# SSD value products in four groups of 32 queries, NSA compression with operands swapped, HGRN steps spread wider

## The chip, the core and the metric

One core of a Trainium2 chip runs the whole program in one launch. The measure is the device time of that launch in microseconds; lower is better. The engines that matter here are TensorE (PE, matrix products; its weight loads have a row PEld of their own), VectorE (DVE), ScalarE (ACT) and the queue on SyncE (SP) that issues the loads.

## What is computed

A first block of two layers (a feed-forward net, a mixer, a second feed-forward net; the mixer is an SSD scan in layer 0 and a pooling mixer in layer 1) is followed by a second block of two layers, in which an HGRN2 recurrence and a native sparse attention (NSA) share the projections of one input. There are 256 tokens (and 256 context tokens in the first block) of width 1024, all in float32. The change touches three places:

```python
# SSD, per chunk of 128, direction and group of 8 heads:
cb = jnp.einsum('bclgn,bcsgn->bclsg', Cc, Bc)
y_diag = jnp.einsum('bclsg,bclsge,bcsgep->bclgep', cb, Lmat, xdt)

# HGRN2, per chunk: decayed scores of queries and keys, then values
attn = jnp.einsum('bhtk,bhsk,bhtsk->bhts', q_, k_, jnp.exp(diff))
o_intra = jnp.einsum('bhts,bhsv->bhtv', attn, v_)

# NSA compression: 15 blocks of 32 tokens, step 16, for each of 2 groups
idx = jnp.arange(n_cmp)[:, None] * CMP_STRIDE + jnp.arange(CMP_BLOCK)[None, :]
blocks = kv[:, idx] + pos_emb[None, None, :, None, :]
flat = blocks.transpose(0, 1, 3, 2, 4).reshape(B, n_cmp, G, CMP_BLOCK * D)
return jax.nn.silu(flat @ w1 + b1) @ w2
```

## The kernel before

**Dense products.** Nearly all of PE's time goes into projections whose weights are streamed from memory once. A load on SP's queue brings raw float32 weights (`wraw`); `prepare` splits them into a rounded high part on ACT (`whi`, L68) and the rest on DVE (`wlo`, L69); PE then makes each product in three passes (`mm3`, L299 to L301; `tm_chunk`, L1173 to L1175). A feature-major projection tile (`fm_tile`, tile `pfm`) is 24 matmuls of 256 columns; its result leaves the PSUM bank by a DVE multiply with the norm factor.

**Order.** The program is written in generators that are interleaved, and a tile scheduler adds the waits; each engine works its own list in that order. `bank` hands out PSUM banks from three tags: five "mm", two "co", one "st".

**SSD core (`core`, one generator for each of 4 groups of 8 heads).** For two halves i of the queries and two directions `d_` the decay matrix `M[i, d_]` (128 keys x 8 heads x 128 queries) is loaded from memory, turned into exponents on ACT (Relu, L666) or DVE, exponentiated (L700) and multiplied by the scores (`cbm`). There are four M buffers in all, so the next group's load waits for the last reader of a buffer. The last reader is `py` (L725): for each head and direction one matmul with the 128x128 piece of M as weights and 64 columns of `xd` moving. Then `yt` takes the sum on DVE (L727), is transposed (`pgy`), gated, and its squares are summed for a norm: `stacc`, `stsq` on ACT and DVE, then `st` on PE (L340). The generators of the groups run beside the projections of the next ones (`px`, `pz`, `pB`, `pC`).

**HGRN2 (`hgrn(half)`, 4 heads each).** Nine terms `(128, 0, 16, 8, 4, 2, 1, 64, 32)` are worked in a pipeline of three steps: `prepare` (DVE makes `z` from the cumulated decays, ACT exponentiates it, DVE multiplies queries and keys in, L1277 to L1287), `score` (PE makes `ps` from z; L1296 for the far term, L1308 for the near terms in four tiles of 32, L1331 for 64 and 32) and `values` (PE, `po`). Near scores are collected in `near` by a multiply with a mask (L1314) and predicated copies (L1317), then spread into `at` (L1323) before the term 64 is scored. After the last term come a sum of squares on PE (`st`, L1365), Ln and exp on ACT, and `on` on DVE (L1367).

**NSA.** `project_nsa` makes `ck` and `cv` (256 tokens for each of 2 groups, with 32 position vectors behind them), then runs `project_more` (keys, values, gates and queries, tiles `kk`, `vv`, `png`, `nq`, with a rope after every second one) with a side chain: `compress("k")`, `compress("v")`, `compressed_out()`, one side step for every second main step (`between`). `compress` adds 32 matmuls in two groups of 16 into `pc`: the weight is `w1[:, j, :]` (128 columns), and 45 columns move (15 blocks of either group, and the position vectors). Each has a bias (`cb`, L1396) and a silu (`s1`, L1398). `compressed_out` makes the compressed keys (`pkc`, `kcmp`, their rope through `pkr`) and values (`vrep`, `pvc`, `vc`). The attention (`nsa`) starts with copies of `kcmp` into `kk` (L1512) and the first scores `psc` (L1532).

**The interleaving.** `run_with(main, side, per)` takes one step of the main generator (the last four query projections of HGRN, then `project_nsa`) and then `per` steps of the side generator (both HGRN halves) on the mean:

```python
run_with(chain(project_q(range(4, 8)), project_nsa()), chain(hgrn(0), hgrn(1)), 2.6)
```

Of the kernel before, what the change touches and what calls it, by code (L numbers as in the profile page):

```python
# [10 lines left out]
F32 = mybir.dt.float32  # L11
# [6 lines left out]
P = 128  # L18
T = 256
# [70 lines left out]
def build(ctx: ExitStack, tc, a, out):  # L90
# [22 lines left out]
    def nm(s):  # L113
        uid[0] += 1
        return f"{s}{uid[0]}"
# [284 lines left out]
    def run_with(main_steps, side_steps, per):  # L400

        due = 0.0
        for _ in main_steps:
            due += per
            while due >= 1.0:
                due -= 1.0
                next(side_steps, 0)
        for _ in side_steps:
            pass

    def ssd_phase(uh, ul, Rx, norm, tail):
        with tc.tile_pool(name="ssd", bufs=1) as sp:
# [234 lines left out]
            def core(g):  # L647
# [55 lines left out]
                for i in range(2):  # L703
                    po = []
                    for d_ in range(2):
                        po.append(bank("co", nm("pyo")))
                        TE.matmul(po[d_], CT[:, P * i:P * i + P], Hst[d_][i ^ d_], start=True, stop=True)
                    xd = [weighted(X[:, 2 + i, :], dt[:, 2 + i, hs[d_]]) for d_ in range(2)]
                    yield
                    yv = yt[:, i, :]  # L710
                    V.tensor_tensor(heads(yv), heads(po[0]), col64(ea[:, i, hs[0]]), op=OP.mult)
                    t = sp.tile([P, 512], F32, tag="xw", name=nm("yx"), bufs=4)
                    V.tensor_tensor(heads(t), heads(po[1]), col64(ea[:, i, hs[1]]), op=OP.mult)
                    V.tensor_add(yv, yv, t)
                    yield
                    for d_ in range(2):
                        V.tensor_tensor(M[i, d_], M[i, d_], cbm[d_][:, i:i + 1, :].to_broadcast([P, 8, P]), op=OP.mult)
                        yield
                    t = weighted(X[:, 2 + i, :], dsk[:, 8 * g:8 * g + 8])
                    V.tensor_add(yv, yv, t)  # L720
                    yield
                    py = bank("co", nm("py"))
                    for h in range(8):
                        for d_ in range(2):
                            TE.matmul(py[:, 64 * h:64 * h + 64], M[i, d_][:, h, :], xd[d_][:, 64 * h:64 * h + 64],  # L725
                                      start=d_ == 0, stop=d_ == 1)
                    V.tensor_add(yv, yv, py)  # L727
                    yield

# [448 lines left out]
    def fm_tile():  # L1178
        p = bank("mm", nm("pfm"))
        dense_tile(p[:, :T], W.next(), 0, KD, xh, xl, T)  # L1180
        return p[:, :T]
# [11 lines left out]
    def block2(l, norm, tail):  # L1193
        if True:
# [59 lines left out]
            def hgrn(half):  # L1254
# [34 lines left out]
                def score(m):  # L1289
                    c = terms[m]  # L1290
                    p = bank("mm", nm("ps"))
                    z = zs.get(m)
                    if c == P:
                        pv = p.rearrange("p (h t) -> p h t", t=P)
                        for h in range(4):
                            TE.matmul(pv[:, h], z[:, h, :P], z[:, h, P:], start=True, stop=True)  # L1296
                        sc["far"] = mx.tile([P, 4, P], F32, tag="h2", name=nm("far"), bufs=4)
                        S.activation(sc["far"], pv, AF.Copy)
                        return
                    if c < 32:  # L1300

                        for h in range(4):
                            for i in range(2):
                                for b in range(4):
                                    ts = slice(P * i + 32 * b, P * i + 32 * b + 32)
                                    lk, lq = ((z[:, h, ts], z[:, h, ts]) if c else
                                              (kT[:, h0 + h, ts], qT[:, h0 + h, ts]))
                                    TE.matmul(p[32 * b:32 * b + 32, 64 * h + 32 * i:64 * h + 32 * i + 32], lk, lq,  # L1308
                                              start=True, stop=True)
                        pv = p[:, :256].rearrange("p (n t) -> p n t", t=32)  # L1310
                        sh = [P, 8, 32]
                        if not c:
                            sc["near"] = mx.tile([P, 8, 32], F32, tag="near", name=nm("near"), bufs=2)
                            V.tensor_tensor(sc["near"], pv, own.unsqueeze(1).to_broadcast(sh), op=OP.mult)  # L1314
                        else:
                            n = PAIRS.index(c)
                            V.copy_predicated(sc["near"], pairs[:, n:n + 1, :].to_broadcast(sh), pv)  # L1317
                        return
                    if c == 64:

                        sc["at"] = mx.tile([P, 8, P], F32, tag="h2", name=nm("at"), bufs=4)
                        sh = [P, 8, 4, 32]
                        V.tensor_tensor(sc["at"].rearrange("p n (b t) -> p n b t", t=32),  # L1323
                                        sc["near"].unsqueeze(2).to_broadcast(sh),
                                        hmask.unsqueeze(1).unsqueeze(3).to_broadcast(sh), op=OP.mult)
                    n = P // (2 * c)
                    for h in range(4):
                        for i in range(2):
                            for e in range(n):
                                k0 = 2 * c * e  # L1330
                                TE.matmul(p[k0:k0 + c, c * (2 * h + i):c * (2 * h + i) + c],  # L1331
                                          z[:, h, P * i + k0:P * i + k0 + c], z[:, h, P * i + k0 + c:P * i + k0 + 2 * c],
                                          start=True, stop=True)
                    for e in range(n):
                        ks, qs = slice(2 * c * e, 2 * c * e + c), slice(2 * c * e + c, 2 * c * e + 2 * c)
                        S.activation(sc["at"][ks, :, qs], p[ks, :8 * c].rearrange("p (n t) -> p n t", t=c), AF.Copy)
# [44 lines left out]
            def compress(s):  # L1381

                x = nt["c" + s]
                w1 = None
                p = bank("mm", nm("pc1"))
                for e in range(2):
                    w1 = mx.tile([P, 16, P], F32, tag="kt", name=nm("w1"))
                    nc.sync.dma_start(w1, a["w1_" + s][l][:, 16 * e:16 * e + 16])
                    yield
                    for j in range(16):  # L1390

                        TE.matmul(p[:, :45], w1[:, j, :], bass.AP(tensor=x.tensor, offset=x.offset + 16 * e + j,
                                                                  ap=[x.ap[0], [T, 3], [16, 15]]),
                                  start=e == 0 and j == 0, stop=e == 1 and j == 15)
                b = mx.tile([P, 1], F32, tag="cb" + s, name=nm("cb"))
                V.tensor_add(b, p[:, 30:31], small["b1_" + s])  # L1396
                s1 = mx.tile([P, 30], F32, tag="s1" + s, name=nm("s1"), bufs=1)
                S.activation(s1, p[:, :30], AF.Silu, bias=b)  # L1398
                nt["s1" + s] = s1

            def compressed_out():

                reps = []
                for g in range(2):
                    r = mx.tile([P, 4, 32], F32, tag="vrep", name=nm("vrep"), bufs=2)
                    V.memset(r, 0.0)
                    V.tensor_copy(r[:, :, :15], nt["s1v"][:, 15 * g:15 * g + 15].unsqueeze(1).to_broadcast([P, 4, 15]))
                    reps.append(r)
# [27 lines left out]

            def project_nsa():
                for s in "kv":
                    t = mx.tile([P, 3, T], F32, name=nm("c" + s), tag="c" + s)
                    nt["c" + s] = t  # L1440
                    nc.sync.dma_start(t[:, 2, :32], a["pos_" + s][l])
                    V.memset(t[:, 2, 32:], 0.0)
                    for g in range(2):
                        V.tensor_mul(t[:, g], fm_tile(), R)
                        yield
                yield from between(project_more(), chain(compress("k"), compress("v"), compressed_out()), 2)

# [39 lines left out]
                S.activation(gates, p[:, :48], AF.Sigmoid)  # L1487
                nt["gates"] = gates

            run_with(chain(project_q(range(4, 8)), project_nsa()), chain(hgrn(0), hgrn(1)), 2.6)  # L1490


            gT = [(xh[:, :, T + 4:], xl[:, :, T + 4:]), (xh[:, :, :T], xl[:, :, :T])]
# [329 lines left out]
```

## Time and profile before

| what | us |
|---|---|
| median of 3 runs | 1966.04 |
| lowest and highest run | 1956.83, 1968.94 |
| profiled execution, its own time | 1965.64 |
| its span in the profile | 1963.9 |
| PE busy in it | 1914.9 |
| DVE busy | 1451.9 |
| ACT busy | 1042.0 |

The span is what the trace covers; its own time is 1.7 us longer. SSD's stretch lies at about 405 to 745 us of the span, the two HGRN/NSA stretches at about 1400 to 1500 (layer 0 of the second block) and 1718 to 1820 (layer 1). A float32 matmul shows as two records, so counts of records are twice the counts of matmuls. A record's own length covers its way through the array and overlaps its neighbours; what it costs PE is the distance from start to start. PEclk, the granted clock, is 1.00 at 2.4 GHz and 0.50 at 1.2 GHz.

### The profile page before, as it was taken

Reading aid. Unit: us, or ns where it says so; the run is one execution under the profiler, and the core shown is the slowest. Engines: PE = TensorE matmul, PEld = TensorE weight load, DVE = VectorE, ACT = ScalarE, POOL = GpSimd, SP = SyncE. Lnnn points to the kernel's source line nnn. Section 1 sums busy time; section 2 is a strip of 40 time slices with the busy share of each in tenths; the row PEclk is TensorE's granted clock in tenths of the full one; section 3 lists DMA queues with packets and bytes.
Section 4 is the critical chain, followed back from the end, with each engine's and each line's share of the span. In section 5 each row is a group of like instructions: output and inputs, shape, how many; then the busy total and the mean of one; then the engine's idle time right before and its main releaser. Section 6 shows DMA issues by size and latency. Waiting matters only on the chain.

```text
span 1963.9 us, 35899 instructions
## 1 busy us (share of the span) xinstructions
PE 1914.9 (98%) x14800; PEld 1744.2 (89%) x14800; DVE 1451.9 (74%) x2683; ACT 1042.0 (53%) x1629; POOL 0.2 (0%) x4
## 2 busy tenths in 40 slices
PE   8999999999999999999999999999999999989998
PEld 3888888897777799999999999999999998989987
DVE  5897788678887789865776587666776856586874
ACT  5332222366766666554555455557554756655573
POOL 0000000000000000000000000000000000000000
PEclk9999999999999999999999999999999999999999
DMA  7767788544323338645554545556434353525332
GB/s 314 260 240 285 274 310 320 186 141 132 88 71 143 107 129 324 245 161 204 178 188 163 203 148 175 171 195 192 152 125 168 108 169 133 194 70 197 133 108 87
DMA packets 81924, 353.03 MB, mean 180 GB/s; under 512 B 12416, under 2 KB 30912, under 8 KB 51040
## 3 DMA queue, kind: packets, MB, share of 16 engines
q1 hardware_dynamic: 81760, 350.73, 51.5%
q8 instruction: 116, 1.90, 0.4%
q14 instruction: 48, 0.39, 0.1%
HBM read 348.80 MB, written 1.12 MB: 178 GB/s over the span
## 4 chain that ended last, share of the span: by engine, by line
PE 89%; DVE 4%; ACT 4%; DMA 2%; issue 1%; SPq 0%; DVEq 0%; ACTq 0%
PE po L299 6%; PE po L301 6%; PE po L300 6%; PE pg L301 5%; PE pu L301 5%; PE pg L300 5%; PE pu L300 5%; PE pg L299 5%; PE pu L299 5%; PE pfm L299 3%; PE pfm L300 3%; PE pfm L301 3%; PE ptm L1173 2%; PE ptm L1174 2%; PE ptm L1175 2%; DMA M<-arow_d 2%
## 5 line engine op out<-in xcount | busy, mean ns | idle before, releaser
L68 ACT ACTIVATE whi<-wraw 128x1024 fp32r<-128x1024 f32 (+1 forms) x485 | 504.2, 1041 | 694.5 <-PE po L300 195.8
L69 DVE TENSOR_TENSOR wlo<-wraw,whi 128x1024 fp32r<-128x1024 f32 (+1 forms) x485 | 581.1, 1199 | 185.9 <-ACT whi L68 184.7
L301 PE MATMUL pg<-xh,wlo 128*128 128x258 f32 (+1 forms) x704 | 219.9, 312 | 0.1
L301 PE MATMUL pu<-xh,wlo 128*128 128x258 f32 (+1 forms) x704 | 219.9, 312 | 0.0
L300 PE MATMUL pg<-xl,whi 128*128 128x258 f32 (+1 forms) x704 | 219.0, 311 | 0.0
L299 PE MATMUL pg<-xh,whi 128*128 128x258 f32 (+1 forms) x704 | 218.5, 311 | 0.4 <-ACT xh L367 0.4
L300 PE MATMUL pu<-xl,whi 128*128 128x258 f32 (+1 forms) x704 | 218.7, 311 | 0.0
L300 PE MATMUL po<-hl,whi 128*128 128x256 f32 (+1 forms) x704 | 218.6, 311 | 0.0
L299 PE MATMUL po<-hh,whi 128*128 128x256 f32 (+1 forms) x704 | 218.6, 311 | 0.0
L301 PE MATMUL po<-hh,wlo 128*128 128x256 f32 (+1 forms) x704 | 218.6, 311 | 0.0
L299 PE MATMUL pu<-xh,whi 128*128 128x258 f32 (+1 forms) x704 | 218.2, 310 | 0.0
L234 DVE SCALAR_TENSOR_TENSOR adascr<-adaraw,csb 128x1024 f32<-128x1024 f32 x152 | 185.7, 1222 | 26.6 <-DMA adaraw<-in_ada 24.6
L299 PE MATMUL pfm<-xh,whi 128*128 128x256 f32 x640 | 189.3, 296 | 0.0
L300 PE MATMUL pfm<-xl,whi 128*128 128x256 f32 x640 | 184.6, 288 | 0.0
L301 PE MATMUL pfm<-xh,wlo 128*128 128x256 f32 x640 | 182.1, 285 | 0.0
L299 PEld LDWEIGHTS pg<-xh,whi 128*128 128x128 f32 x704 | 133.6, 190 | 8.6 <-ACT xh L367 0.6
L300 PEld LDWEIGHTS po<-hl,whi 128*128 128x128 f32 x704 | 133.8, 190 | 8.1
L301 PEld LDWEIGHTS po<-hh,wlo 128*128 128x128 f32 x704 | 133.8, 190 | 8.1
L299 PEld LDWEIGHTS po<-hh,whi 128*128 128x128 f32 x704 | 133.8, 190 | 8.1
L299 PEld LDWEIGHTS pu<-xh,whi 128*128 128x128 f32 x704 | 133.6, 190 | 7.8
L300 PEld LDWEIGHTS pg<-xl,whi 128*128 128x128 f32 x704 | 133.0, 189 | 7.9
L301 PEld LDWEIGHTS pg<-xh,wlo 128*128 128x128 f32 x704 | 132.9, 189 | 8.1 <-DVE wlo L69 0.3
(444 smaller groups left out, 4233.5 us busy)
## 6 DMA issues: line engine op xcount, KB each, us to landing
wraw<-in_ffn_gu SPq DMA_DIRECT2D x88, 1024.0 KB, 4.9
adaraw<-in_ada SPq DMA_DIRECT2D x64, 1024.0 KB, 6.5
wraw<-in_w SPq DMA_DIRECT2D x60, 1024.0 KB, 4.9
wraw<-in_ffn_d SPq DMA_DIRECT2D x24, 960.0 KB, 4.7
wraw<-in_ssd_wi SPq DMA_DIRECT2D x20, 1024.0 KB, 4.9
wraw<-in_w_out SPq DMA_DIRECT2D x16, 1024.0 KB, 5.1
wraw<-in_ffn_d SPq DMA_DIRECT2D x24, 448.0 KB, 3.2
adan<-in_ada_n SPq DMA_DIRECT2D x8, 1024.0 KB, 7.7
```

Source lines behind the costliest of these rows:

```text
L68: nc.scalar.activation(hi[:, :n], raw[:, o:o + n], AF.Copy)
L69: nc.vector.tensor_sub(lo[:, :n], raw[:, o:o + n], hi[:, :n].bitcast(F32))
L234: V.scalar_tensor_tensor(scr, t[:, h, :], 1.0, csb[s], op0=OP.mult, op1=OP.mult, accum_out=macc[l, s][:, n:n + 1])
L299: TE.matmul(o, wh, xh, start=start, stop=False)
L300: TE.matmul(o, wh, xl, start=False, stop=False)
L301: TE.matmul(o, wl, xh, start=False, stop=stop)
L1173: TE.matmul(o, h, wh[:, sl], start=k == 0, stop=False)
L1174: TE.matmul(o, h, wl[:, sl], start=False, stop=False)
L1175: TE.matmul(o, l, wh[:, sl], start=False, stop=k == KD - 1)
```

## The change

In SSD each of the 16 matmuls of `py` becomes four, with 32 query columns of M as weights each, which write 32 partitions of the result. In the compression the operands change places: 32 columns of x (step 16, both groups and the position columns) are the weights, `w1` (128 columns) moves, and four tokens j go into four groups of 32 partitions. The four partial sums are copied out by ACT (`part`), a yield follows, and one more matmul with the matrix `own` adds them in a new bank (`pc2`). For that the layout of `ck` and `cv` changes, and each projection tile leaves by two multiplies of 240 columns where one of 256 was. `near` has one buffer for two; `vrep` lies in another pool under the tag of `stsq`. `run_with` takes 1.9 side steps per main step for 2.6.

```diff
+                            for q in range(0, P, 32):
+                                TE.matmul(py[q:q + 32, 64 * h:64 * h + 64], M[i, d_][:, h, q:q + 32],
+                                          xd[d_][:, 64 * h:64 * h + 64], start=d_ == 0, stop=d_ == 1)
-                            TE.matmul(py[:, 64 * h:64 * h + 64], M[i, d_][:, h, :], xd[d_][:, 64 * h:64 * h + 64],
-                                      start=d_ == 0, stop=d_ == 1)
...
-                            sc["near"] = mx.tile([P, 8, 32], F32, tag="near", name=nm("near"), bufs=2)
+                            sc["near"] = mx.tile([P, 8, 32], F32, tag="near", name=nm("near"), bufs=1)
...
-                        TE.matmul(p[:, :45], w1[:, j, :], bass.AP(tensor=x.tensor, offset=x.offset + 16 * e + j,
-                                                                  ap=[x.ap[0], [T, 3], [16, 15]]),
-                                  start=e == 0 and j == 0, stop=e == 1 and j == 15)
+                        q = 32 * (j % 4)
+                        TE.matmul(p[q:q + 32, :P], bass.AP(tensor=x.tensor, offset=x.offset + 496 * e + j,
+                                                           ap=[x.ap[0], [16, 32]]),
+                                  w1[:, j, :], start=e == 0 and j < 4, stop=e == 1 and j > 11)
+                part = tmp.tile([P, P], F32, tag="t1k", name=nm("part"), bufs=2)
+                S.activation(part, p[:, :P], AF.Copy)
+                yield
+                p = bank("mm", nm("pc2"))
+                TE.matmul(p[:, :32], part, own, start=True, stop=True)
                 b = mx.tile([P, 1], F32, tag="cb" + s, name=nm("cb"))
-                V.tensor_add(b, p[:, 30:31], small["b1_" + s])
+                V.tensor_add(b, p[:, 15:16], small["b1_" + s])
...
-                    r = mx.tile([P, 4, 32], F32, tag="vrep", name=nm("vrep"), bufs=2)
+                    r = tmp.tile([P, 4, 32], F32, tag="stsq", name=nm("vrep"), bufs=2)
...
                     for g in range(2):
-                        V.tensor_mul(t[:, g], fm_tile(), R)
+                        p = fm_tile()
+                        for e in range(2):
+                            V.tensor_mul(t[:, e, 256 * g:256 * g + 240], p[:, 16 * e:16 * e + 240],
+                                         R[:, 16 * e:16 * e + 240])
...
-            run_with(chain(project_q(range(4, 8)), project_nsa()), chain(hgrn(0), hgrn(1)), 2.6)
+            run_with(chain(project_q(range(4, 8)), project_nsa()), chain(hgrn(0), hgrn(1)), 1.9)
```

How the lists of instructions move is shown at three places. The first is PE at the end of the first HGRN half of layer 0: `ps` are scores, `pfm` with its `whi` a projection tile, of which the first of its 24 rows stands here, `po` the values. Before:

```order
L1308 MATMUL ps1304_14446<-z21299_14367 32x32 x32
L1308 MATMUL ps1306_14485<-z21301_14407 32x32 x32
L299 MATMUL pfm1307_14519<-xh_93,whi356_14336 128x256
...
L1308 MATMUL ps1309_14557<-z21305_14480 32x32 x32
L299 MATMUL pfm1311_14594<-xh_93,whi357_14417 128x256
...
L1331 MATMUL ps1313_14630<-z21308_14551 64x64 x8
L1331 MATMUL ps1315_14642<-z21312_14624 32x32 x16
L299 MATMUL pfm1316_14661<-xh_93,whi358_14520 128x256
...
L1347 MATMUL po1286_14173<-at1314_14631,vt1272_13824 128x128 x4
```

And now:

```order
L1310 MATMUL ps1305_14864<-z21301_14785 32x32 x32
L299 MATMUL pfm1307_14901<-xh_93,whi357_14755 128x256
...
L1310 MATMUL ps1309_14937<-z21304_14858 32x32 x32
L299 MATMUL pfm1310_14971<-xh_93,whi358_14826 128x256
...
L1310 MATMUL ps1312_15010<-z21308_14932 32x32 x32
L299 MATMUL pfm1314_15045<-xh_93,whi359_14902 128x256
...
L1333 MATMUL ps1316_15081<-z21311_15004 64x64 x8
L299 MATMUL pfm1318_15093<-xh_93,whi360_14972 128x256
...
L1333 MATMUL ps1322_15134<-z21315_15075 32x32 x16
L299 MATMUL pfm1323_15153<-xh_93,whi361_15046 128x256
...
L1349 MATMUL po1286_14557<-at1317_15082,vt1272_14208 128x128 x4
```

Before, six projection tiles stand from the near scores of the first term (`ps1293`) to the values, and twice two scores follow each other directly; now each score has a tile behind it, and the values stand nine tiles after the far scores.

The second place is DVE just ahead of the attention of layer 0. `nq` and `z` are projections leaving their banks, `rsw` and `nq` the steps of a rope, `kcsw` and `kcmp` that of the compressed keys, `vcmp` the masked compressed values. Before:

```order
L69 TENSOR_TENSOR wlo377_15675<-wraw201_15426,whi377_15674 128x1024
L1502 TENSOR_TENSOR vcmp1395_15742<-vc1383_15592,b_head_mask_13393 128x512
L1475 TENSOR_TENSOR nq1365_15366<-pfm1388_15637,rstd_2_13492 128x256
L1424 TENSOR_TENSOR kcsw1390_15669<-pkr1389_15667,b_ropec_s_13381 32x30
L1425 TENSOR_TENSOR kcmp1382_15590<-kcmp1382_15590,b_ropec_c_13379 32x30
L69 TENSOR_TENSOR wlo378_15714<-wraw202_15525,whi378_15713 128x1024
L1189 TENSOR_TENSOR rsw1387_15631<-rsw1387_15631,b_rope_s_13377 32x512
L1190 TENSOR_TENSOR nq1365_15366<-nq1365_15366,b_rope_c_13375 32x512
L1426 TENSOR_TENSOR kcmp1382_15590<-kcmp1382_15590,kcsw1390_15669 32x30
L1475 TENSOR_TENSOR nq1365_15366<-pfm1391_15673,rstd_2_13492 128x256
L1191 TENSOR_TENSOR nq1365_15366<-nq1365_15366,rsw1387_15631 32x512
L1512 COPY kk1321_14716<-kcmp1382_15590 128x15 x2
```

And now:

```order
L1516 TENSOR_TENSOR vcmp1399_16138<-vc1392_16094,b_head_mask_13777 128x512
L1369 SCALAR_TENSOR_TENSOR on1280_14518<-po1332_15263,b_hnorm_13779,r1379_15997 128x512
L1433 TENSOR_TENSOR kcsw1396_16103<-pkr1395_16101,b_ropec_s_13765 32x30
L1434 TENSOR_TENSOR kcmp1391_16092<-kcmp1391_16092,b_ropec_c_13763 32x30
L1516 TENSOR_TENSOR vcmp1399_16138<-vc1392_16094,b_head_mask_13777 128x512
L1435 TENSOR_TENSOR kcmp1391_16092<-kcmp1391_16092,kcsw1396_16103 32x30
L69 TENSOR_TENSOR wlo379_16159<-wraw202_15797,whi379_16158 128x1024
L1191 TENSOR_TENSOR rsw1389_16084<-rsw1389_16084,b_rope_s_13761 32x512
L1192 TENSOR_TENSOR nq1348_15542<-nq1348_15542,b_rope_c_13759 32x512
L1642 TENSOR_TENSOR z1397_16107<-pfm1398_16108,rstd_2_13876 128x256
L1193 TENSOR_TENSOR nq1348_15542<-nq1348_15542,rsw1389_16084 32x512
L1526 COPY kk1313_15044<-kcmp1391_16092 128x15 x2
```

The copy into `kk` now stands behind the last `on` of HGRN, which was 34 rows ahead of it before, and behind a `z` that comes from the projection tile after `pkr`.

The third is PE at the same place, with `pkr` (the rope product of the compressed keys) and `psc` (the first scores of the attention); of each projection tile the first row stands here. Before:

```order
L1392 MATMUL pc11352_15236<-cv1310_14591,w11367_15413 128x45 x16
L299 MATMUL pfm1378_15520<-xh_93,whi371_15422 128x256
...
L299 MATMUL pfm1380_15558<-xh_93,whi372_15465 128x256
...
L1411 MATMUL pkc1381_15588<-s11351_15234,wc2_k1282_14137 128x30
L1418 MATMUL pvc1384_15593<-wc2_v1284_14141,vrep1376_15514 128x128
L1418 MATMUL pvc1385_15596<-wc2_v1284_14141,vrep1377_15517 128x128
L299 MATMUL pfm1386_15599<-xh_93,whi373_15521 128x256
...
L299 MATMUL pfm1388_15637<-xh_93,whi374_15559 128x256
...
L1422 MATMUL pkr1389_15667<-kcmp1382_15590,b_rot_13383 32x30
L299 MATMUL pfm1391_15673<-xh_93,whi375_15600 128x256
...
L299 MATMUL pfm1394_15712<-xh_93,whi376_15638 128x256
...
L1532 MATMUL psc1399_15751<-kk1321_14716,nq1365_15366 128x143
```

And now:

```order
L1402 MATMUL pc21382_16034<-own_13784,part1372_15916 128x32
L1367 MATMUL st1387_16047<-sq1378_15996,ones_91 128x512
L299 MATMUL pfm1388_16052<-xh_93,whi375_15931 128x256
...
L1420 MATMUL pkc1390_16090<-s11352_15577,wc2_k1282_14521 128x30
L1427 MATMUL pvc1393_16095<-wc2_v1284_14525,vrep1385_16040 128x128
L1427 MATMUL pvc1394_16098<-wc2_v1284_14525,vrep1386_16043 128x128
L1431 MATMUL pkr1395_16101<-kcmp1391_16092,b_rot_13767 32x30
L299 MATMUL pfm1398_16108<-xh_93,whi376_16005 128x256
...
L1546 MATMUL psc1403_16147<-kk1313_15044,nq1348_15542 128x143
```

From the last sum of the compressed values to the first `psc` there were six projection tiles, two of them behind `pkr`; now there are two, one of them behind `pkr`.

## Rows read from the trace of the kernel before

The timeline joins neighbouring records of one kind into one row, with their count; a matmul's shapes are weights (rows * columns) and then the result.

**Rows 1.** The page: busy time of the engines, and the chain's shares by engine.

```profile
PE 1914.9 (98%) x14800; PEld 1744.2 (89%) x14800; DVE 1451.9 (74%) x2683; ACT 1042.0 (53%) x1629; POOL 0.2 (0%) x4
...
PE 89%; DVE 4%; ACT 4%; DMA 2%; issue 1%; SPq 0%; DVEq 0%; ACTq 0%
```

**Rows 2.** Table of stretches: us, busy by engine, then PEclk, DMA share, GB/s.

```profile
405.00:745.00 340.00, 323.04 (x1975) 273.86 (x1974) 278.94 (x465) 234.91 (x418) 0.00 (x0) 0.98 0.36 120
1400.00:1500.00 100.00, 94.76 (x1500) 89.16 (x1499) 74.59 (x119) 52.90 (x66) 0.00 (x0) 0.95 0.38 131
1428.00:1430.00 2.00, 2.00 (x11) 2.00 (x11) 0.00 (x0) 0.54 (x2) 0.00 (x0) 0.50 0.72 299
1486.00:1490.00 4.00, 4.00 (x19) 2.97 (x18) 0.00 (x0) 0.84 (x2) 0.00 (x0) 0.61 0.44 119
```

**Rows 3.** The chain around one py call: start us, length us, what.

```profile
634.14 3.52 PE py L725 x32
```

**Rows 4.** Timeline of PE, scores of layer 0: start us, us; idle before in brackets.

```profile
1417.47 0.75 PE L1308 MATMUL ps<-z 128*32 128x32 f32 x64 [0.91 <-DVE z L1283]
...
1421.68 1.12 PE L1331 MATMUL ps<-z 128*64 128x64 f32 x16 [0.43 <-DVE z L1285]
1426.69 1.07 PE L1331 MATMUL ps<-z 128*32 128x32 f32 x32 [3.89 <-DVE z L1285]
...
1475.93 1.77 PE L1331 MATMUL ps<-z 128*64 128x64 f32 x48
1477.63 0.38 PE L299 MATMUL pfm<-xh,whi 128*128 128x256 f32 x1
```

**Rows 5.** Timeline of PE, the far scores and first near scores of layer 0.

```profile
1399.00 0.28 PE L301 MATMUL pfm<-xh,wlo 128*128 128x256 f32 x1
1399.12 1.05 PE L1296 MATMUL ps<-z 128*128 128x128 f32 x8
1400.10 0.76 PE L1308 MATMUL ps<-qT,kT 128*32 128x32 f32 x64
1400.79 0.39 PE L299 MATMUL pfm<-xh,whi 128*128 128x256 f32 x1
```

**Rows 6.** Timeline of PE, a compression group and the scores behind it.

```profile
1451.48 3.68 PE L1392 MATMUL pc<-ck,w 128*128 128x45 f32 x32
1455.09 1.36 PE L1308 MATMUL ps<-z 128*32 128x32 f32 x128
1456.39 0.39 PE L1173 MATMUL ptm<-whi,xh 128*128 128x256 f32 x1
```

**Rows 7.** The chain in the SSD stretch, after a py call.

```profile
509.01 3.10 PE py L725 x29
512.11 5.19 DMA M<-arow_d
```

**Rows 8.** PE's waits in layer 1: us in total, times, longest us.

```profile
PE ps L1331 <- DVE z L1285: 4.3, 2, 3.9
PE ps L1308 <- DVE z L1283: 0.7, 1, 0.7
```

**Rows 9.** The chain on DVE in layer 0: start us, us to the next.

```profile
1422.46 0.60 DVE z L1279
1423.06 1.14 DVE at L1323
1424.20 1.14 DVE wlo L69
```

**Rows 10.** Timeline of all engines, the last steps before the attention of layer 0.

```profile
1496.72 1.28 ACT L1398 ACT_TABLE_LOAD   x1
...
1515.65 0.23 DVE L1512 COPY kk<-kcmp 128x15 f32<-128x15 f32 x2
...
1517.11 0.40 PE L1532 MATMUL psc<-kk,nq 128*128 128x143 f32 x2
```

**Rows 11.** Timeline of ACT and PE in the SSD stretch, around one norm sum.

```profile
592.16 0.69 ACT L666 ACTIVATE M<-M,acol 128x128 f32<-128x128 f32 x2 [7.54 <-DMA M<-arow_d]
...
597.51 1.22 PE L340 MATMUL st<-stacc,ones 128*128 128x256 f32 x2 [4.85 <-DVE stacc L333]
```

More of the change, by code (lines that the diff above doesn't have):

```diff
@@ L1383, in compress @@
                 x = nt["c" + s]
-                w1 = None
                 p = bank("mm", nm("pc1"))
@@ L1390, in compress @@
                     for j in range(16):
-                        TE.matmul(p[:, :45], w1[:, j, :], bass.AP(tensor=x.tensor, offset=x.offset + 16 * e + j,
-                                                                  ap=[x.ap[0], [T, 3], [16, 15]]),
-                                  start=e == 0 and j == 0, stop=e == 1 and j == 15)
+                        q = 32 * (j % 4)
[7 more added lines that the diff above has]
+                TE.matmul(p[:, :32], part, own, start=True, stop=True)
                 b = mx.tile([P, 1], F32, tag="cb" + s, name=nm("cb"))
-                V.tensor_add(b, p[:, 30:31], small["b1_" + s])
+                V.tensor_add(b, p[:, 15:16], small["b1_" + s])
                 s1 = mx.tile([P, 30], F32, tag="s1" + s, name=nm("s1"), bufs=1)
-                S.activation(s1, p[:, :30], AF.Silu, bias=b)
+                S.activation(s1.rearrange("p (g n) -> p g n", g=2),
+                             p[:, :32].rearrange("p (g n) -> p g n", g=2)[:, :, :15], AF.Silu, bias=b)
                 nt["s1" + s] = s1
@@ L1438, in project_nsa @@
                 for s in "kv":
-                    t = mx.tile([P, 3, T], F32, name=nm("c" + s), tag="c" + s)
+                    t = mx.tile([P, 1008], F32, name=nm("c" + s), tag="c" + s)
                     nt["c" + s] = t
-                    nc.sync.dma_start(t[:, 2, :32], a["pos_" + s][l])
-                    V.memset(t[:, 2, 32:], 0.0)
+                    V.memset(t[:, 992:], 0.0)
+                    t = t[:, :992].rearrange("p (e n) -> p e n", e=2)
+                    nc.sync.dma_start(t[:, :, 240:256], a["pos_" + s][l].rearrange("p (e j) -> p e j", e=2))
                     for g in range(2):
-                        V.tensor_mul(t[:, g], fm_tile(), R)
+                        p = fm_tile()
+                        for e in range(2):
+                            V.tensor_mul(t[:, e, 256 * g:256 * g + 240], p[:, 16 * e:16 * e + 240],
+                                         R[:, 16 * e:16 * e + 240])
                         yield
```

## The prediction

> **What bounds it now.** I read the page's busy shares first, then the chain, then a table by stretch, then single rows. TensorE (PE) is busy 98% of the span and holds 89% of the chain [rows 1]: a microsecond taken from PE's own stream is a microsecond of the end, if PE has work behind it. In the three stretches that the change touches this holds less strictly: PE is busy 323 of 340 us in the SSD stretch and 95% in the HGRN/NSA stretch of layer 0, where DVE is busy 75% and ACT 53% [rows 2]. Times are set against the profiled run (1965.64 us, span 1963.9, so 1.7 us lies around the span); the median of the runs is 1966.04, 0.4 above it, which I neglect.
>
> **1. SSD value products.** Each of the 8 calls of py runs 16 matmuls as 32 records. One call that is not broken up lies on the chain for 3.52 us [rows 3], 110 ns per record, though 64 moving columns need less: 16 records of 64x64 in one tile last 1.12 us [rows 4], with some 0.2 us for the end of the last one about 60 ns per record. So the 128-column weight sets the 110 ns, not the stream. The change cuts each weight into four of 32 columns on four column groups: 128 records per call, each still with 64 moving columns. What four groups cost is in the trace, at half this width: 64 records with 32-column weights and 32 moving columns start at 1400.10 and the next fm tile at 1400.79, 0.69 us or 10.8 ns per record, 43 ns for four [rows 5]; 128 of them take 1.30 us (1455.09 to 1456.39, [rows 6]), 41 ns for four. Hence four do run beside each other. With 64 moving columns four cannot be faster than one such stream, 60 ns, so a call is 32 x 60 ns = 1.92 us. Entering and leaving costs something: the first fm matmul after such a run is 0.39 instead of 0.28 us long, I take 0.2 us per call. Gain 3.52 - 2.12 = 1.4 us, times 8 = **-11.2 us**. Bounds: four at 43 ns as in the row, 1.38 us a call, -15.5; no concurrency, 128 x 60 ns = 7.7 us a call, +35. The rows are nearest to the first, so I stay at 60 ns. The gain counts in full because the call is on PE's stream and the chain goes through it, and behind it the next M load waits for its end: 3.10 us of py, then 5.19 us of DMA M [rows 7].
>
> **2. Compression.** Before, each layer compresses k and v in two groups of 16 matmuls (32 records) each: 8 groups in all, like the one that starts at 1451.48 with the next work at 1455.09 [rows 6]; less 0.1 for the switch to four tiles behind it that is 3.52 us, again 110 ns per record, for 45 moving columns behind a 128-column weight. After, x is the weight (32 columns, four groups) and w1 moves (128 columns). A 128-column record is 110 ns: 8 of them in 1.05 us [rows 5], of which 0.28 are the last one's own length. Four at once: 8 x 111 = 0.9 us, plus 0.2 for the switch, 1.1. Gain 2.42 x 8 = -19.4. The new sum over partial results is one matmul of 32 columns per compression, about 0.2 us with its pipe, 4 x 0.2 = +0.8. The ACT copy of 128x128 ahead of it costs PE nothing: ACT is busy 53 of 100 us there [rows 2], and a yield, so at least one projection tile of 2.8 us, lies between the copy and the sum; uncovered it would cost its half microsecond four times. Sum **-18.6**. Bounds: two at a time 1.78 + 0.2 us a group, -12.3 + 0.8 = -11.5; none beside each other, 3.52 + 0.2, +2.4. Behind one of the 8 groups (1483.45) the granted clock fell: 0.61 on the mean from 1486 to 1490 [rows 2], a loss of 4 x 0.39 = 1.6 us that I let go with the group: **-1.6**. The split of the c tiles costs DVE two multiplies of 240 columns for one of 256, a third of a microsecond eight times over both layers; it lies on DVE and is in the next step.
>
> **3. HGRN spread, 2.6 to 1.9.** Before, the first half's last scores stand directly behind each other on PE: six fm tiles between the far scores and the values, while DVE has work for more: PE idles 0.91, 0.43 and 3.89 us for DVE's z [rows 4], 5.2 us; layer 1 has two of 4.3 us together, the longest 3.9 [rows 8], and one of 0.7, 5.0 us. Behind the long one the clock is at 1.2 GHz (0.50, [rows 2]) for some 4 us in layer 0 and 3 us in layer 1, half of it lost: 2.0 and 1.6 us. Removable: 10.2 + 3.6 = -13.8. The new order puts nine fm tiles there. The last score has eight of them ahead of it: 24 records of 0.117 us each, 2.82 us a tile [rows 5], 22.6 us, with six scores of 0.7, one of 1.0 and values of 0.94 some 28.7 us of PE. DVE has for the same stretch 26 z steps of 0.60 us, 6 wlo and one at of 1.14 [rows 9], and 6 near steps and 11 projection multiplies of a third of a microsecond each: 29.2 us. DVE starts behind, with two wlo of the tiles before still to do, so I leave 1.7 us of idle: +3.4 over two layers.
>
> The other end is where the spread has its price. HGRN's second half now ends where compressed_out ends, and compress has a third step, so pkc, pvc and pkr move towards the attention. Before, six fm tiles stand between the last pc group and the first psc, two of them after pkr, and PE goes from one to the next with no idle (psc at 1517.11 carries no idle, the copy into kk that it needs is at 1515.65, [rows 10]). After, two fm tiles are left, pfm1388 and pfm1398, and the copy into kk stands on DVE behind the last "on" (which needs Ln, a table load of 1.28 us [rows 10] and an exp on ACT), two vcmp, a wlo, three rope steps and a multiply. Walking the two lists by durations from pkr: ACT's load and exp end 2.3 us later, "on" 0.67, kcsw and kcmp 0.2, vcmp 0.6, wlo 1.2 (its whi has waited for the same ACT list), rope and z 2.1, copy 0.3: 7.3 us; PE has 2.9 us of work. So a **new PE wait of 4.4 us in front of psc**, per layer: +8.8, and, as behind the 3.89 us wait, 1.8 us of low clock each: +3.6. Net of step 3: -13.8 + 3.4 + 8.8 + 3.6 = **+2.0**. If ACT's table load and exp come early enough for the wait to vanish, it is -10.4; a wait twice as long, for a late whi, makes it +10.8.
>
> **4. Buffers** (near to one, vrep into stsq's tag): near is rewritten once per half, after at has read it; between them lie several fm tiles. Nothing. ACT's list in SSD also changes: stacc and stsq come ahead of the M Relus that wait for DMA M, where before they stood behind one that waited 7.54 us, and PE idled 4.85 us for stacc [rows 11]. That could give another -4.9 and some clock behind it, but the same wait can reappear one row later, in front of sz; I count 0.
>
> **Sum**: 1965.6 - 11.2 - 18.6 - 1.6 + 2.0 = 1936.2, **1936**.
>
> **A rule weighed.** The four-group row gives 10.8 ns from record to record [rows 5]. The Trainium skill, "TensorE: Matmul & The Clock Gate", section "Wait — 56ns, not 53.3ns?", has matmuls never closer than about 25 ns however small they are; this trace does not agree for four column groups. By it a py call would be 128 x 25 = 3.2 us, the gain of step 1 some 1 us instead of 11, and the time 1946, an estimate from that page.
>
> **Rivals.**
> B, the tail is covered. ACT runs ahead, the wait in front of psc is under 1 us. For it: ACT is busy only half of these stretches [rows 2]. Against: table loads and Ln, exp stand between two silus in the new list. 1936 - 12.4 = 1924; with the stacc wait gone too, 1916.
> C, a record costs at least 23 ns. The two-tile row shows it: 48 records from 1475.93 to 1477.63, 1.70 us, of which 16 one-tile ones take 0.96, leaves 23 ns for each of 32 [rows 4]. Then py is 128 x 23 = 2.95 us, 3.0 instead of 11.2 gained: 1944. Against it stand the 10.8 ns.
> C2, only two groups run beside each other when the moving stream is wide. py 64 x 60 = 3.84 + 0.2, +4.2 in place of -11.2; pc -11.5 in place of -18.6: 1936 + 15.4 + 7.1 = 1959. The rows of four have 32 moving columns only and cannot exclude it.
> D, slower: the moving streams of the four groups follow each other, since each record brings its own 64 columns. py 7.7 us a call, +35; pc +2.4, and the clock's 1.6 us stays; with step 3's +2.0, 1965.6 + 35 + 2.4 + 2.0 = 2005. It decides from 110 ns for four records on; the rows have 43.
>
> **Chances.** The forecast A 0.46, B 0.24, C 0.09, C2 0.10, D 0.04; 0.07 lies between A and no change (the tail wait longer than walked, about 1947). The predicted time is A's. The range reaches from B with half of the stacc gain, 1920, to half-way from C to C2, 1952; A's own is 1929 to 1943. About 1% (1946.4) is what a measurement here can tell from no change: faster holds A, B, C and part of the rest, 0.80; within 1% C2 and the rest, 0.16; slower 0.04.
>
> **What would show it.** py calls of about 2.1 us each, 1.9 for four records of 60 ns; pc groups of about 1.1 us; PE waits for z L1285's line under 2 us per layer; a PE wait of some 4 us before the first psc of each layer with "kk" as the releaser, followed by clock 0.50. Step 1 is wrong if py stays near 3 us, step 2 if pc is near 2, step 3 if psc has no wait or the half-one waits remain. The forecast fails as a whole if the SSD stretch does not shorten by what py loses, that is if DMA M or ACT sets it.

## The result

| kernel | median us | lowest to highest | runs |
|---|---|---|---|
| before | 1966.2 | 1956.83 to 1968.94 | 4 |
| changed | 1930.14 | 1928.23 to 1930.6 | 4 |

The ratio is 0.9819 (95% interval 0.9804 to 0.9834): the change takes 36 us off. The forecast was 1936 with a range of 1920 to 1952.

### The profile page after: what moved, and what is told of

Read it like the earlier page. It is cut to its first block, busy times and chain, and to the rows that moved or that the text cites. A ratio compares the mean times of both kernels' runs of the same rounds, so it can differ in the third digit from the quotient of the medians.

```text
span 1928.5 us, 37463 instructions
## 1 busy us (share of the span) xinstructions
PE 1883.5 (98%) x15576; PEld 1707.2 (89%) x15576; DVE 1453.0 (75%) x2691; ACT 1047.4 (54%) x1637; POOL 0.2 (0%) x4
## 4 chain that ended last, share of the span: by engine, by line
PE 87%; ACT 5%; DMA 3%; DVE 2%; issue 1%; SPq 0%; DVEq 0%; ACTq 0%
PE po L299 6%; PE po L301 6%; PE po L300 6%; PE pg L301 5%; PE pu L301 5%; PE pg L300 5%; PE pu L300 5%; PE pg L299 5%; PE pu L299 5%; PE pfm L299 4%; PE pfm L300 4%; PE pfm L301 3%; PE pw L300 2%; PE pw L299 2%; PE pw L301 2%; PE ptm L1175 2%
## 5 line engine op out<-in xcount | busy, mean ns | idle before, releaser
L234 DVE SCALAR_TENSOR_TENSOR adascr<-adaraw,csb 128x1024 f32<-128x1024 f32 x152 | 185.6, 1221 | 18.0 <-DMA adaraw<-in_ada 15.9
```

The lines of the kernel that those rows point to most:

```text
L234: V.scalar_tensor_tensor(scr, t[:, h, :], 1.0, csb[s], op0=OP.mult, op1=OP.mult, accum_out=macc[l, s][:, n:n + 1])
```

## The profile after

The page of the changed kernel, the lines that answer to [rows 1], and its span (profiled execution: 1930.26 us):

```profile
span 1928.5 us, 37463 instructions
...
PE 1883.5 (98%) x15576; PEld 1707.2 (89%) x15576; DVE 1453.0 (75%) x2691; ACT 1047.4 (54%) x1637; POOL 0.2 (0%) x4
...
PE 87%; ACT 5%; DMA 3%; DVE 2%; issue 1%; SPq 0%; DVEq 0%; ACTq 0%
```

PE holds as much of the span as before (98%). It is busy 31 us less and the span is 35.4 us shorter. Where that lies is seen from the times at which the same steps start on PE, read from the timelines of both kernels (us; the last `pgy` is its last row):

| step | before | changed | gained in the stretch |
|---|---|---|---|
| last `pgy` (SSD's products are done) | 724.8 | 710.0 | 14.8 |
| first `ps`, layer 0 | 1399.1 | 1384.4 | -0.1 |
| first `psc`, layer 0 | 1517.1 | 1489.7 | 12.7 |
| first `ps`, layer 1 | 1717.4 | 1691.9 | -1.9 |
| first `psc`, layer 1 | 1833.4 | 1796.0 | 11.9 |
| end | 1963.9 | 1928.5 | -2.0 |

All of the gain is in the three stretches that the change touches, and behind each of the two NSA starts some of it is given back.

The value products, in the timeline of PE of the changed kernel (start us, length us, operation); this call answers to [rows 3]:

```profile
624.51 1.99 PE L727 MATMUL py<-xw,M 128*32 128x64 f32 x128
626.43 0.50 PE L299 MATMUL px<-xh,whi 128*128 128x512 f32 x1
```

From 624.51 to 626.43 are 1.92 us for 128 records: 15.0 ns per record, 60 ns for four. From start to start, all eight calls together take 16.2 us of PE's stream, 27.8 before.

A compression group and the last sum, the same view; they answer to [rows 6]:

```profile
1425.79 1.11 PE L1395 MATMUL pc<-w,ck 128*32 128x128 f32 x32
1426.83 0.39 PE L1175 MATMUL ptm<-whi,xh 128*128 128x256 f32 x1
...
1448.37 0.30 PE L1402 MATMUL pc<-own,part 128*128 128x32 f32 x2
1448.60 0.76 PE L1310 MATMUL ps<-z 128*32 128x32 f32 x64
```

This group takes 1.04 us where one took 3.6, the sum 0.23 us. All eight groups take 7.9 us of PE's stream, 28.4 before, and the four sums 0.7 us.

PE's waits (us in total, times, longest us), first around layer 0's HGRN and NSA, then around layer 1's; they answer to the idle times in [rows 4] and to [rows 8]:

```profile
PE psc L1546 <- DVE kk L1526: 3.8, 1, 3.8
PE pfm L300 <- issue: 1.2, 1, 1.2
...
PE psc L1546 <- DVE kk L1526: 3.9, 1, 3.9
PE psc L1546 <- ACT pt L1590: 0.3, 1, 0.3
```

The waits of the scores for z are gone altogether. A new wait of 3.8 and 3.9 us stands in front of the first psc, for the copy into kk. The 1.2 us in front of `pfm`, put down to "issue", that is to nothing that the profile names, are taken up in the last section. What follows the wait for kk, by stretches of the changed kernel (us, busy by engine, then PEclk, DMA share, GB/s):

```profile
1384.40:1489.70 105.30, 100.18 (x1657) 93.65 (x1655) 93.03 (x156) 64.12 (x80) 0.00 (x0) 1.00 0.44 154
1489.00:1493.00 4.00, 3.31 (x15) 3.31 (x16) 2.13 (x7) 0.49 (x2) 0.00 (x0) 0.50 0.59 238
1795.00:1799.00 4.00, 2.99 (x13) 2.99 (x14) 2.45 (x8) 0.49 (x2) 0.00 (x0) 0.62 0.61 242
```

Up to the wait the granted clock is 1.00 on the mean; behind it, it is 0.50 (1.2 GHz) in layer 0 and 0.62 on the mean in layer 1. From the first psc to the first transposition behind it (`pct`) layer 0 takes 24.2 us where it took 21.3, layer 1 23.1 for 21.3: 4.7 us together.

In the SSD stretch one wait is all but gone, which [rows 11] showed at 4.85 us and which before came to 6.8 us in three pieces (PE's waits from 405 to 745, the first line of the kernel before, the others of the changed kernel):

```profile
PE st L340 <- DVE stacc L333: 6.8, 3, 4.8
...
PE pgy L741 <- ACT X L634: 2.1, 2, 1.3
PE ph L677 <- DVE xw L644: 1.8, 2, 1.0
...
PE py L727 <- DVE M L717: 1.4, 1, 1.4
...
PE st L340 <- DVE stacc L333: 0.6, 2, 0.4
```

## Experiments

Every kernel ran in three rounds beside the kernel before, and ratios are to it. First the three parts apart.

**Value products alone.** The kernel before, with these lines:

```diff
-                            TE.matmul(py[:, 64 * h:64 * h + 64], M[i, d_][:, h, :], xd[d_][:, 64 * h:64 * h + 64],
+                            for q in range(0, P, 32):
+                                TE.matmul(py[q:q + 32, 64 * h:64 * h + 64], M[i, d_][:, h, q:q + 32], ...
```

> The kernel before with the four-group py alone. Theory (PE's stream, and what hangs on it): a py call falls from 3.52 to about 1.92 us, 8 x 1.6 = 12.8 us, and PE's wait of 4.8 us for stacc in the SSD stretch goes too, because ACT's list changes with py alone: about 1949 to 1952 us. Rival (the M loads and ACT set the SSD stretch): PE's gain comes back as longer waits for M, the stretch shortens by under 5 us: about 1962. The HGRN and NSA stretches stay as before in both.

Measured: 1947.97 us against 1963.85, ratio 0.9915 (0.9896 to 0.9935): 15.9 us. The last pgy is at 709.3, 15.5 us earlier than before, and the waits for z are unchanged (4.2 and 1.0 us in layer 0). So the SSD stretch gives what PE's stream loses (11.6 us) and some 3.9 us more; the wait for stacc falls from 6.8 to 1.4 us, while those of pgy and ph grow by some 2 us. Single profiles scatter by almost 2 us here, but the eight kernels that run py once in four groups have their last pgy at 708.5 to 710.4, and the three with the py of before at 724.8 to 726.6. The stretch is not set by the M loads.

**The compression alone**, with 2.6 steps:

> Only the compression (new layout, operands swapped, extra yield; near and vrep as changed) in the kernel before, with 2.6 steps. Theory: each of 8 groups falls from 3.52 to about 1.04 us, 4 sums of about 0.25 us come on top, -19; the three waits for z in each first half stay (10 us in all); in front of the first psc there is one projection tile behind pkr, but no norm step of HGRN ahead of the copy on DVE, so a wait of at most 1 us: about 1947. Rival (the extra yield alone makes the wait in front of psc): 4 us per layer with the low clock behind it, about 1957.

Measured: 1949.05 us, ratio 0.9919 (0.9901 to 0.9936): 14.8 us, 4 less than the theory. The interval reaches from 12.6 to 19.4 us, so the times alone do not tell the two apart. The profile says more: from the first ps to the first pct the layers are 9.1 and 5.7 us shorter, while the groups and sums take some 20 us less of PE's stream. PE's waits around layer 0:

```profile
PE ps L1331 <- DVE z L1285: 4.7, 2, 4.2
PE ps L1308 <- DVE z L1283: 1.3, 1, 1.3
PE pvc L1425 <- DVE vrep L1414: 0.7, 1, 0.7
PE pb L1233 <- ACT bT L1237: 0.4, 1, 0.4
PE ps L1308 <- DVE z L1285: 0.3, 1, 0.3
```

The waits for z add up to 6.3 us (5.2 before), and pvc waits 0.7 us for vrep. In layer 1 it is 5.6 us for z (5.0 before), 0.7 for vrep and 0.7 put down to issue, so the waits of both layers have grown by 3.8 us. In the first half, where DVE finishes last, projection tiles now leave by two multiplies of 240 columns instead of one of 256, a third of a microsecond more each, and three of the four in layer 0 lie ahead of its last scores. That fits the 1.1 us there, but no run takes these multiplies away by themselves. A wait in front of psc does not occur, so the rival is out.

**The spread alone**, 1.9 for 2.6 in the kernel before:

> Only 1.9 for 2.6 in the kernel before. Theory (spread pays, the price at the tail comes only with the compression's extra yield): the waits for z (10.2 us) and the low clock behind them (3.6 us) go, two projection tiles still stand behind pkr, so the wait in front of psc is under 1.5 us: about 1953. Rival (the spread alone makes the wait, because the last norm step of HGRN comes ahead of the copy into kk): about 4 us of wait and 1.8 of clock per layer: about 1963.

Measured: 1953.35 us, ratio 0.9935 (0.9914 to 0.9956): 10.5 us. No wait for z is left in either layer, and none in front of psc: the stretches from the first ps to the first psc are 7.2 and 6.5 us shorter, 13.7 together; the SSD stretch, which has the same code, came out 1.5 us longer.

**Both, without the spread.** The changed kernel with 2.6:

> The changed kernel with 2.6 for 1.9. Theory: py and compression as in the changed kernel, the waits for z are back (10 us and 3.6 of low clock), and the wait in front of psc is nearly gone, since HGRN's last norm step is early again: about 1931 to 1934, so the spread is worth little by itself beside this tail. Rival (the wait in front of psc stays, it is the extra yield's): about 1943.

Measured: 1935.52 us, ratio 0.9853 (0.9834 to 0.9873); the changed kernel is 5.4 us faster. Its waits around layer 0:

```profile
PE ps L1333 <- DVE z L1287: 4.9, 2, 4.2
PE ps L1310 <- DVE z L1285: 1.2, 1, 1.2
PE pb L1235 <- ACT bT L1239: 0.7, 1, 0.7
PE pvc L1427 <- DVE vrep L1416: 0.7, 1, 0.7
PE ps L1310 <- DVE z L1287: 0.2, 1, 0.2
```

The waits for z are back (6.3 us) and psc waits for nothing: pkr has one projection tile behind it here too, but no HGRN step stands between on DVE. So neither the spread alone nor the compression's third step alone makes the wait in front of psc. It takes both: the one puts HGRN's end there, the other the compression's.

**Taking the wait away, in three ways.** The changed kernel without the third step's yield:

```diff
                 S.activation(part, p[:, :P], AF.Copy)
-                yield
                 p = bank("mm", nm("pc2"))
```

> The changed kernel without the yield between the copy of the partial sums and their last sum; compressed_out comes two steps earlier, with two more projection tiles ahead of the first psc. Theory: the wait in front of psc (3.8 us a layer) and the low clock behind it (1.8 us) go, -11; but PE now waits for the copy on ACT, 4 times up to 1.5 us: about 1920 to 1925. Rival (the wait in front of psc is not the yield's, but stands behind HGRN's last norm step): the wait stays over 2.5 us and the waits for the copy come on top: about 1933.

Measured: 1920.31 us, ratio 0.9763 (0.9738 to 0.9788). The wait for kk is gone, and the last sum waits for the copy only 0.4 and 0.6 us in the two layers.

The yield kept, but the compression stepped faster:

```diff
-                for n, _ in enumerate(steps):
-                    if n % every == every - 1:
+                due = 0.0
+                for _ in steps:
+                    due += 1.0
+                    if due >= every:
+                        due -= every
                         next(side, 0)
...
-                yield from between(project_more(), chain(compress("k"), compress("v"), compressed_out()), 2)
+                yield from between(project_more(), chain(compress("k"), compress("v"), compressed_out()), 1.5)
```

> The changed kernel with the yield kept, but with a side step of the compression for every 1.5 projection steps, not 2, so that it ends as early as without the yield. Theory: no wait in front of psc, and no wait for the copy: about 1919. Rival as in the kernel without the yield: the copy into kk still stands behind HGRN's last norm step, the wait stays over 2.5 us: about 1930.

Measured: 1918.38 us (1916.95 to 1918.59), ratio 0.9757 (0.9731 to 0.9783). It beats both kernels, the changed one by 11.8 us. From psc to pct it takes 21.3 us in both layers, as before, so the low clock went with the wait. The forecast's rival B, 1924, is what the change gives with its tail covered, and a little more. PE's waits around layer 0:

```profile
PE pb L1235 <- ACT bT L1239: 1.2, 1, 1.2
PE ps L1310 <- issue: 0.3, 1, 0.3
PE psc L1549 <- ACT pt L1593: 0.3, 1, 0.3
PE prc L1158 <- DVE rstd L1101: 0.2, 1, 0.2
```

With a step for every projection step:

> The same with a side step of the compression for every projection step: pkr comes about nine projection tiles ahead of the first psc. Theory: nothing of the compression is late any more; if a wait in front of psc is left, it is for something else (the queries, HGRN): about 1919, as with 1.5. Rival: compression and HGRN crowd ACT and DVE earlier, the waits for z come back by some us: about 1925.

Measured: 1918.51 us, ratio 0.9762 (0.9737 to 0.9786), the same. Two tiles behind pkr are enough.

**What the spread is worth without that wait.** The kernel with 1.5, and 2.6 HGRN steps:

> The kernel with a compression step for every 1.5 projection steps, and 2.6 HGRN steps in place of 1.9: what the spread is worth where the attention does not wait for the compression. Theory: the waits for z (11 to 12 us over both layers, as in the changed kernel with 2.6) and the low clock behind them (3.6 us) come back: about 1932. Rival (part of the gain of the 1.5 was the earlier compression filling PE in the second half): under 8 us, about 1925.

Measured: 1931.66 us, ratio 0.9829 (0.9815 to 0.9844): 13.3 us slower than with 1.9. So the spread is worth 13 us here, of which the tail takes back 8 in the changed kernel. Not all of the 13 us is the waits for z and the clock: 3.0 us of PE's waits in layer 1 are put down to issue, of which the theory knew nothing (see the last section):

```profile
PE ps L1333 <- DVE z L1287: 4.9, 2, 4.2
PE ps L1310 <- issue: 3.0, 2, 2.4
```

With 2.2:

> The same with 2.2 HGRN steps: HGRN ends earlier, and the first half has one pair of scores directly behind each other again. Theory (DVE sets the first half): a wait for z of 1 to 2 us comes back in each layer, about 1921. Rival (seven tiles before the last score are cover enough): no wait, about 1917.

Measured: 1924.49 us, ratio 0.979 (0.9775 to 0.9804), 6.1 us slower than with 1.9. Waits for z of 1.8 and 1.5 us are back in the two layers, as the theory has it. The rest is not in it: pauses of PE that are put down to issue (1.3 us in layer 0, 2.4 in layer 1).

**What a group of columns costs.** The changed kernel with py in two groups of 64 queries:

> The changed kernel with py in two groups of 64 queries instead of four of 32. Theory (the moving stream sets the pace once the weights are narrow enough to load beside it): 32 pairs of 60 ns, 1.9 us a call, the same time as the changed kernel, 1930. Rival (a weight load of n columns always costs its n columns on PE, and only the four-group mode hides it): 64 records at 55 to 60 ns, 3.5 us a call: about 1943.

Measured: 1934.7 us, ratio 0.9839 (0.9817 to 0.9861). In its timeline the call that stood alone above is:

```profile
629.46 2.08 PE L727 MATMUL py<-xw,M 128*64 128x64 f32 x64
631.47 0.50 PE L299 MATMUL px<-xh,whi 128*128 128x512 f32 x1
```

2.01 us for 64 records, against 1.92 for 128: two records take the time that four took. The theory on the mechanism holds: once the weights are 64 columns or fewer, the 64 moving columns set the pace. The 4.6 us that the kernel is slower are not in the products (17.0 us for all calls, 16.2 in the changed kernel) but in waits elsewhere in the SSD stretch, 3.3 us of them for one cv, after the scheduler had put the steps in another order.

**Is the length of py what counts in SSD?** Each product made twice, the second overwriting the first, in four groups:

```diff
-                        for d_ in range(2):
+                        for d_ in (0, 1, 0, 1):
                             for q in range(0, P, 32):
```

> The changed kernel with each value product made twice (the second run of both directions overwrites the first), so that a py call costs 64 x 60 ns = 3.84 us in four groups. Theory (PE's stream decides in SSD, the call's length is what counts): +8 x 1.92 = 15.4 us in the SSD stretch, about 1945. Rival (M loads and ACT set the stretch, PE's length is hidden behind them): under 6 us, about 1934.

Measured: 1958.52 us, ratio 0.997 (0.9955 to 0.9984): 28.4 us more than the changed kernel, beyond either expectation. PE's waits in the SSD stretch and one call in the timeline:

```profile
PE py L727 <- issue: 10.5, 7, 2.8
```

```profile
639.61 2.99 PE L727 MATMUL py<-xw,M 128*32 128x64 f32 x196
643.67 1.09 PE L727 MATMUL py<-xw,M 128*32 128x64 f32 x60 [1.08 <-issue]
```

After 196 records in 3 us PE stands for 1.08 us and the profile names nothing that it waits for; seven such pauses, in six of the eight calls, make 10.5 us, the longest 2.8. Together with 15.7 us of longer calls that is 26.2 of the 28.4 us. To tell whether the pauses come from the number of instructions or from the work, the same doubled work in two groups, with half as many instructions:

> Each value product made twice (the second run overwrites the first), in two groups of 64 queries: the same 3.84 us of moving columns per py call as with four groups twice, with half as many instructions. Theory (with four groups twice, PE idled 10.5 us with nothing that it waited for after some 200 records at 15 ns: instructions come slower than that): no such idle, +8 x 1.9 = 15 against two groups once (1934.7): about 1950. Rival (the idle is the value products' own, for M or for the bank): it stays, about 1958.

Measured: 1945.84 us, ratio 0.9894 (0.9878 to 0.9911), 15.7 us above the changed kernel, whose calls take 15.4 us less; 11.1 above the two groups once, whose calls take 14.6 us less but which has the 3.3 us of wait for cv that do not occur here.

```profile
631.33 3.95 PE L727 MATMUL py<-xw,M 128*64 128x64 f32 x128
635.22 0.50 PE L299 MATMUL px<-xh,whi 128*128 128x512 f32 x1
```

A call of 128 records lasts 3.9 us and no pause is left. So the length of py does set the stretch, and the pauses belong to the stream of instructions, not to the work. This kernel is also a control for the SSD stretch: its calls are longer than those of before (3.9 for 3.5 us) and its last pgy is still at 724.0 (724.8 before), with 0.9 us of wait for stacc where before had 6.8. On ACT's list stacc and stsq stand ahead of the late M's Relus in it too, so the shorter wait comes with that order and not with the shorter py.

## The prediction, step by step

**Step 1, value products: right.** Four records in 60 ns is what the stream does. A call that stands alone takes 1.92 us, without the 0.2 us for entering and leaving; one that other work splits in two takes 2.06. All calls together lose 11.6 us where 11.2 was predicted.

**ACT's list in SSD, counted at 0: partly wrong.** The wait for stacc went, 6.2 us. Its reappearance "one row later" is partly seen: pgy's and ph's waits grew. The stretch gained 14.8 us in all, 11.6 of it in py's stream, so about 3 us stayed.

**Step 2, compression: right.** 0.93 to 1.04 us a group for 1.1 expected, the sum 0.14 to 0.23 for 0.2: -20.5 and +0.7 us where -19.4 and +0.8 were predicted. The clock term (1.6) is in the mean of 1.00 above. Alone, the compression gave 14.8 us in its run, since PE's waits grew; the added multiplies on DVE, where DVE is the bound, explain a part of that. The prediction saw them as part of step 3, where the spread covers them.

**Step 3, first half: right in mechanism, too cautious.** All waits for z went, 10.2 us and the clock behind them, and none of the 3.4 us that I left stayed. Half a microsecond of DVE against PE was within the error of that walk.

**Step 3, tail: right, and slightly too long.** Predicted 4.4 us per layer before psc for kk, measured 3.8 and 3.9. The chain in front of it, in the changed kernel (start us, length us):

```profile
1478.83 1.28 ACT L1406
...
1480.13 0.29 ACT s L1406
...
1480.43 1.28 ACT L358
...
1481.72 0.69 ACT r L358
...
1482.68 1.28 ACT L359
...
1483.98 0.64 ACT r L359
...
1484.64 0.75 DVE on L1369
...
1486.28 1.13 DVE wlo L69
1487.41 0.60 DVE rsw L1191
...
1489.55 0.10 DVE kk L1526
```

Here is the walk: three table loads of 1.28 us stand on ACT one after another, for silu, Ln and exp, then "on", then wlo and the rope on DVE, then the copy. From pkr at 1482.60 to psc at 1489.69 it is 7.1 us, where I had 7.3; PE ran for 3.3 us of it, where I had 2.9. The clock behind it cost 4.7 us (3.6 predicted). The prediction gave two causes, the spread and the third step, in one sentence; the experiments show that either alone makes no wait.

**The sum.** -11.6 (py), -3.2 (rest of SSD), -20.5 and +0.7 (compression), -1.6 (clock), -13.8 (waits for z and the clock behind them), +7.7 and +4.7 (tail), +1.2 (the pause in layer 0 put down to issue) make -36.4, where the span has -35.4; 1.0 us is spread over small waits that no run singles out. The forecast was some 6 us short, most of it because it left idle time in the first half (3.4 us) and nothing for the new order in SSD (3.2 us).

**The rivals.** C (23 ns per record) and C2 (two at a time) fall by the 15.0 ns per record, D with them. The rule weighed, from the Trainium skill, "TensorE: Matmul & The Clock Gate", section "Wait — 56ns, not 53.3ns?", that matmuls are never closer than about 25 ns, does not hold for four column groups at 64 moving columns either: they come every 15.0 ns. B describes the kernel with the tail covered, which the change is not. B's second figure, 1916, takes 8 us off for stacc, where [rows 11] shows 4.85 and the waits of before come to 6.8; 4.9 would have given 1919.

## What to carry to other kernels

When a weight load of 128 columns is longer than the stream that it serves, cutting the weight into column groups lets four products share one stream's time; the pace to expect is that of the moving columns (here 60 ns for four records at 64), and two groups of 64 columns get nearly the same with half the instructions. That counts in long runs: 512 instructions in a row at this pace outran their fetching in six calls of eight. When two chains of small steps are spread over one main chain, look at where both end: neither shift alone made a wait there, both together put a chain of table loads and rope steps in front of the next stage, and ending one chain earlier, so that two projection tiles stand behind its last product and not one, was worth as much as a third of the whole change. A saving read from one engine's stream holds only where the engine that is next (here DVE in the first HGRN half) has room, so the parts do not add up to the whole in either direction.

## What was not expected of the hardware

PE's stream can be too dense for the fetching of its instructions. At 15.0 ns per record (each a weight load and a matmul, so two instructions) calls of 128 records ran without a pause, but in calls of 256 records PE stood still seven times, for 1.0 to 2.8 us, in six calls of eight, and not at all in the calls with the same work at 30 ns per record. The waits name no releaser, but the trace shows what PE stood for. The profile counts the fetches of instructions on a queue of their own. Here is that queue's row on the page of the kernel with four groups twice, for the whole span (packets, MB, share), and its row for 641.3 to 641.4 us, just ahead of the pause shown above:

```profile
q8 instruction: 130, 2.13, 0.4%
...
q8 instruction: 1, 0.02, 59.4%
```

That is 16 KB a fetch, and one fetch for every 256 instructions of PE and PEld, of which the kernel has 33200. The fetch that starts at 641.33 lands at 642.28, and PE goes on at 643.67. In all seven pauses PE goes on 1.3 to 1.5 us after a fetch has landed, 2.3 to 2.9 us after the fetch began. Counted over the instructions of PE and PEld from the start of the kernel, all seven end at the same place in a block of 256, while in their calls they lie anywhere from 115 to 243 records in. The other 14 pauses of PE that are put down to issue, in ten of the fourteen kernels, end at that same place and equally soon after a fetch: among them the 1.2 us of the changed kernel, the 3.0 us of the kernel with 1.5 and 2.6 steps and the 3.7 us of the one with 2.2. So these are waits for instructions, and where they fall in a dense stretch is a matter of the count, not of the spread. The lengths fit: 256 instructions last 1.92 us at 15.0 ns per record and 3.9 us at 30 ns, and the 2.3 to 2.9 us lie between. The Trainium skill, "Runtime: NRT & Kernel Launch", section "Instruction fetch mechanics", says that fetching is hidden because engines dispatch more slowly than instructions arrive; these pauses do not agree with that for such records.
